# Norm sums by products with ones, rotary sums and 24 convolution taps a layer by accumulating transfers, in a two-layer hybrid encoder

## The chip, the cores and the metric

The kernel runs on one core of a Trainium2 chip. The metric is the device time of one execution in microseconds. A core has a matrix engine (TensorE, PE in the profile, PEld for its weight loads), three elementwise engines (VectorE is DVE, ScalarE is ACT, GpSimd is POOL), and 16 DMA engines that are fed by queues; the queues here are SP's (SyncE), POOL's and, rarely, ScalarE's. Each engine works through its own instructions in order and waits on semaphores for the others.

## The reference

Two layers work on x (512 tokens by 1024 channels, float32). Cut to what matters:

```python
h = rmsnorm(x, norm_mix[i])
proj = h @ w_in[i]
qa, ka, va, glu_in, qc, kc, vc, gates = split(proj)
ya = diff_attention(qa, ka, va, ...)      # 4 heads, rotary embedding on q and k, rmsnorm per head
yb = conformer_conv(glu_in, ...)          # gate, 31-tap depthwise convolution, layernorm, silu
yc = neighbourhood_attention(qc, kc, vc, rpb)
ga, gb, gc = split(sigmoid(gates))
x = x + (ga * (ya @ w_br_a) + gb * (yb @ w_br_b) + gc * (yc @ w_br_c)) @ w_o
h = rmsnorm(x, norm_ffn[i])
x = x + (silu(h @ w_ffn_gate) * (h @ w_ffn_up)) @ w_ffn_down
h = rmsnorm(x, norm_ple[i])
x = x + sigmoid(h @ w_ple_gate) * (p[i] @ w_ple_in)
# after both layers: rmsnorm(x, norm_final)

def apply_rope(x, cos, sin):
    x1, x2 = x[..., :half], x[..., half:]
    rot = concatenate([-x2, x1])
    return x * cos + rot * sin
```

## The kernel before

Activations lie transposed: channels on the 128 partitions, the 512 tokens along the row. Every float32 operand of a large product is split into a high and a low part (`split`: ScalarE copies the high part, VectorE subtracts it for the low part, lines L147 and L161), and one product is three matmuls, high by high, high by low and low by high (L181 to L183). Weights come in tiles of 128x1024 on SP's queue, are split the same way, and have three buffers for each of raw, high and low (tags `wr`, `wh`, `wl`).

TensorE's order is written out by hand; the order on the other engines is made by a scheduler from priorities. A counter of product chunks (`chunk`, `tick`) drives generators: attention units, norms and the convolution's end are resumed so many ticks later (`yield n`, `later`), so that their few matmuls lie between those of the large products.

A norm (`norm`, L207 to L233) takes a tile of squares `sq`, 128 partitions by 512 tokens. Four transposes (L217) put tokens on the partitions, VectorE reduces along the row (L220), a small VectorE instruction scales the sum, POOL raises it to the power -0.5 (L227), and after some ticks four more transposes (L231) broadcast the result over the partitions. It is called for each of the six main norms, for the eight heads' norms and for the convolution's two.

The rotary embedding (`diff_in`, L831 on) takes the projection of a head's queries or keys: ScalarE copies it out of PSUM into `raw`, four transfers on SP's queue (L846) write the swapped 32-partition blocks into `rot`, VectorE multiplies `raw` by the cosine table in place and `rot` by the sine table and adds them. Then the sum is split, and `stack` (L664) copies 64-partition pieces into the layout of the scores, four transfers for queries and eight for keys, on SP's queue.

The convolution has 31 taps for each of 4 channel blocks, one VectorE instruction each (`taps`, L164 with `conv_z`). `background` puts so many taps behind given instructions of other stages; the numbers are in `BG` (per call, by stage). The convolution's sums `cs` are finished by `conv`, which begins after `merge_a`.

The order of a layer: `glu` (gate of the convolution), neighbourhood attention's projections and units, the differential attention's `diff_in`, `diff_v` and units, the gates `gate_c`, the branch `branch_c`, `merge_a`, `gate_b`, `merge_b`, the output projection `w_o`, the FFN and the per-layer input. In the FFN, POOL already issues accumulating transfers (L1004), which add weight blocks from DRAM to a tile in SBUF.

Of the kernel before, what the change touches and what calls it, by code (L numbers as in the profile page):

```python
# [14 lines left out]
AF = mybir.ActivationFunctionType  # L15
ALU = mybir.AluOpType
AX = mybir.AxisListType
# [3 lines left out]
P = 128  # L21
# [3 lines left out]
GR = 8  # L25
# [5 lines left out]
CON3W = 31  # L31
# [14 lines left out]
PAR_L = 8 + 8 + 8 + 1 + 4 + 4 + 4 + 4 * CON3W  # L46
PAR = L * PAR_L + 8
WARM = 8
BG = dict(glu=2, natten=1, values=3, diff=1, gatec=2, branchc=2, gateb=4, mergea=4, mergea2=2)
FIRST = (["v"] * 4 + ["pt"] * 2 + ["y", "b"], ["y"] * 5 + ["pt"] * 2 + ["b"])  # L50
EARLY = 6
QUARTERS = (2, 4, 6)
# [13 lines left out]
class Net:  # L66
# [143 lines left out]
    def norm(self, sq, n, waits, done, spread=True, eps=None):  # L210


        nc = self.nc
        yield waits[0]
        st = self.ps("tr", (P, 4, P))
        for c in range(4):
            nc.tensor.transpose(st[:, c, :], sq[:, c * P:(c + 1) * P], self.ident)  # L217
        with self.tc.high_priority(offset=min(200, self.tc.cur_priority - self.p0) if n == D and self.p0 is not None else 0):
            sm = self.sb("sm", [P, 4])
            nc.vector.tensor_reduce(out=sm, in_=st, op=ALU.add, axis=AX.X)  # L220
            ms = self.sb("sm", [P, 4])
            if eps is None:
                nc.vector.tensor_scalar(ms, sm, 1.0 / n, EPS, ALU.mult, ALU.add)
            else:
                self.stt(ms, sm, 1.0 / n, eps, ALU.mult, ALU.add)
            col = self.sb("rc", [P, 4])
            nc.gpsimd.tensor_tensor(col, ms, self.power, ALU.pow)  # L227
        yield waits[1]
        bc = self.ps("tr", (P, 4, P))
        for c in range(4):  # L230
            nc.tensor.transpose(bc[:, c, :], col[:, c:c + 1].to_broadcast([P, P]), self.ident)  # L231
        bc = bc.rearrange("p a b -> p (a b)")
        done(col, self.spread(bc) if spread else bc)  # L233
# [198 lines left out]
    def layer(self, i, h, xsrc, xs):  # L432
        self.i, self.h = i, h
        zs, cs = [], []
        self.todo = self.taps(zs, cs)
        self.glu(zs)
        if i == 0:
            self.lambdas()
        yc, ya, yb = [], [], []
        sn, sd = {}, {}  # L440
        self.natten_in(0, sn, yc)
        self.drain(self.renorm)
        self.h = self.hs
        self.natten_v(sn)
        last = self.glu_last(zs)
        self.natten_in(1, sn, yc)
        next(last)
        self.natten_in(2, sn, yc)
        next(last)
        self.natten_in(3, sn, yc)  # L450
        acc, gb = [], []
        self.diff_in(0, sd, ya)
        self.diff_v(0, sd)
        self.diff_in(1, sd, ya)
        self.gate_c(acc, 0)
        self.diff_in(2, sd, ya)
        self.diff_v(1, sd)
        self.diff_in(3, sd, ya)
        for m in range(1, KD):
            self.gate_c(acc, m)  # L460
        for m in range(2):
            self.gate_b(gb, m, AF.Copy, None)
        for g in acc + gb:
            self.act(g, g, AF.Sigmoid, table="sigmoid")
        self.branch_c(acc, yc)
        for m in range(2, 4):
            self.gate_b(gb, m, AF.Sigmoid, "sigmoid")
# [12 lines left out]
        h = self.ffn(h, x)  # L480
        return self.ple(h, x, xs, self.inputs())
# [57 lines left out]
    def taps(self, zs, cs):  # L539

        for j, z in enumerate(zs):
            zf = z.rearrange("p a b -> p (a b)")
            c = self.sb("z", [P, 512])
            cs.append(c)
            for d in range(CON3W):
                w = self.par(self.i, "cw", j * CON3W + d)
                src = zf[:, d * GR:d * GR + 512]
                if d == 0:
                    yield self.nc.vector.tensor_scalar(c, src, w, self.par(self.i, "cb", j),
                                                       ALU.mult, ALU.add)  # L550
                else:
                    yield self.stt(c, src, w, c, ALU.mult, ALU.add)

    def background(self, after, n):

# [223 lines left out]
    def gate_c(self, acc, m):  # L779
        self.phase = "gatec"  # L780
        ps = self.proj(OFF_G + 2 * D + m * P)
        if m % 2 == 0:
            acc += self.parts_of("x", [512], 2)
        self.background(self.act(acc[m], ps, AF.Copy), self.bg["gatec"])

    def branch_c(self, acc, ys):
        self.phase = "branchc"
        for m in range(KD):
            ps = self.ps("mm")
            self.gemm(ps, self.a["w_br_c"][self.i, m], ys)  # L790
            self.background(self.tt(acc[m], acc[m], ps, ALU.mult), self.bg["branchc"])

    def merge_a(self, ys, acc):
        self.phase = "mergea"
        for m in range(KD):
            ps = self.proj(OFF_G + m * P)
            g = self.sb("t", [P, 512])
            self.background(self.act(g, ps, AF.Sigmoid, table="sigmoid"), self.bg["mergea"])
            pb = self.ps("mm")
            self.gemm(pb, self.a["w_br_a"][self.i, m], ys)  # L800
            self.tt(g, g, pb, ALU.mult)
            self.background(self.tt(acc[m], acc[m], g, ALU.add), self.bg["mergea2"])

    def gate_b(self, gs, m, func, table):
        self.phase = "gateb"
        ps = self.proj(OFF_G + D + m * P)
        if m % 2 == 0:
            gs += self.parts_of("v", [512], 2)
        self.background(self.act(gs[m], ps, func, table=table), self.bg["gateb"])

    def merge_b(self, ys, acc, gs):
        self.phase = "mergeb"
# [17 lines left out]
    def diff_in(self, head, st, ys):  # L830
        self.phase = "diff"  # L831
        if head == 0:
            st["tabs"] = []
            for t in range(2):
                c = self.sb("r", [P, 512])
                self.nc.sync.dma_start(c, self.a["rope"][t])
                st["tabs"].append(c)
        st4 = self.sb("qk", [P, 4, 512], F32R)
        k2 = self.sb("x", [P, 2, 512], F32R)
        for s, off in enumerate((OFF_QA, OFF_KA)):  # L840
            ps = self.proj(off + head * P)
            raw, rot = self.sb("rp", [P, 512]), self.sb("rp", [P, 512])
            self.act(raw, ps, AF.Copy, scale=1.0 if s else 0.125)
            for b in range(4):
                o = b ^ 1
                self.nc.sync.dma_start(rot[32 * b:32 * b + 32], raw[32 * o:32 * o + 32])  # L846
            self.background(self.tt(raw, raw, st["tabs"][0], ALU.mult), self.bg["diff"])
            self.tt(rot, rot, st["tabs"][1], ALU.mult)
            self.tt(raw, raw, rot, ALU.add)
            nat, low = self.sb("kh", [P, 512], F32R), raw.bitcast(F32R)  # L850
            self.split(nat, low, raw)
            self.stack(nat, low, st4[:, 2 * s:2 * s + 2], k2 if s else None)
        box = dict(s0=self.sb("sm", [P, 4]))
        for qt in range(4):
            self.later(self.diff_unit(head, qt, st4, k2, st, box, ys), 6 if head else 7, 2)
# [538 lines left out]
def _token_order():  # L1394
    t = np.arange(S)
    return (t % GR) * GW + t // GR


def _rope_tables():
    inv = np.float32(1.0) / (10000.0 ** (np.arange(0, 64, 2) / 64)).astype(np.float32)  # L1400
    ang = np.arange(S, dtype=np.float32)[:, None] * inv[None, :]
    ang = np.concatenate([ang, ang], axis=-1)
    cos, sin = np.cos(ang), np.sin(ang)
    sin[:, :32] = -sin[:, :32]
    n = _token_order()
    return np.ascontiguousarray(
        np.stack([np.concatenate([c[n].T, c[n].T], axis=0) for c in (cos, sin)])).astype(np.float32)

# [75 lines left out]
```

## Time and profile before

| | us |
|---|---|
| median of 3 runs | 1768.67 (1768.25 to 1769.67) |
| span of the profiled execution, first to last instruction; the page states no other time of it | 1766.6 |
| TensorE busy | 1759.3 |
| VectorE busy | 1408.6 |
| ScalarE busy | 885.5 |
| POOL busy | 98.4 |

The granted clock of TensorE is 1.000 over the span. A row of the page's groups gives line, engine, operation, tile written and tiles read, the shape, the count, then busy time in us, the mean in ns, and idle time before with what ended it. The waits name who waited for whom, with total, count and longest in us. A timeline row begins with start and length in us.

### The profile page before, as it was taken

Reading aid. Unit: us, or ns where it says so; the run is one execution under the profiler, and the core shown is the slowest. Engines: PE = TensorE matmul, PEld = TensorE weight load, DVE = VectorE, ACT = ScalarE, POOL = GpSimd, SP = SyncE. Lnnn points to the kernel's source line nnn. Section 1 sums busy time; section 2 is a strip of 40 time slices with the busy share of each in tenths; the row PEclk is TensorE's granted clock in tenths of the full one; section 3 lists DMA queues with packets and bytes.
Section 4 is the critical chain, followed back from the end, with each engine's and each line's share of the span. In section 5 each row is a group of like instructions: output and inputs, shape, how many; then the busy total and the mean of one; then the engine's idle time right before and its main releaser. Section 6 shows DMA issues by size and latency. Waiting matters only on the chain.

```text
span 1766.6 us, 27127 instructions
## 1 busy us (share of the span) xinstructions
PE 1759.3 (100%) x10146; PEld 1551.8 (88%) x10146; DVE 1408.6 (80%) x2354; ACT 885.5 (50%) x1529; POOL 98.4 (6%) x114
## 2 busy tenths in 40 slices
PE   9999999999999999999999999999999999999998
PEld 7888888888899899998888888888888998989987
DVE  7967988998898587787777688889887976867776
ACT  5576555325565254454545655552356643534444
POOL 0000000000111010100000000000001110101000
PEclk9999999999999999999999999999999999999999
DMA  6575641334757365544446655322356674655332
GB/s 231 158 186 160 162 123 54 102 100 150 222 153 196 106 173 156 137 126 127 151 137 173 180 148 154 108 73 94 101 183 194 168 179 118 172 141 156 99 104 96
DMA packets 112548, 253.95 MB, mean 144 GB/s; under 512 B 14368, under 2 KB 23328, under 8 KB 112416
## 3 DMA queue, kind: packets, MB, share of 16 engines
q1 hardware_dynamic: 99024, 227.83, 42.0%
q0 software_dynamic: 12672, 23.07, 8.1%
q8 instruction: 80, 1.31, 0.3%
q10 hardware_dynamic: 720, 1.31, 0.2%
q14 instruction: 52, 0.43, 0.1%
HBM read 214.41 MB, written 7.34 MB: 126 GB/s over the span
## 4 chain that ended last, share of the span: by engine, by line
PE 92%; DVE 4%; DMA 2%; ACT 2%; issue 1%; SPq 0%; POOL 0%; ACTq 0%; POOLq 0%; DVEq 0%
PE ffn_mm L1034 4%; PE ffn_mm L1036 4%; PE ffn_mm L182 4%; PE ffn_mm L181 4%; PE ffn_mm L183 4%; PE ffn_mm L1035 4%; PE ffn_sc L1036 3%; PE ffn_sc L1034 3%; PE ffn_sc L1035 3%; PE mergea_mm L182 2%; PE mergea_mm L183 2%; PE mergea_mm L181 2%; PE gateb_mm L182 2%; PE gateb_mm L183 2%; PE gateb_mm L181 2%; PE wo_mm L182 2%
## 5 line engine op out<-in xcount | busy, mean ns | idle before, releaser
L164 DVE SCALAR_TENSOR_TENSOR conv_z<-glu_z,pre_par,conv_z 128x512 f32<-128x512 f32 x240 | 179.6, 748 | 3.5
L147 ACT ACTIVATE ffn_wh<-ffn_wr 128x1024 fp32r<-128x1024 f32 (+1 forms) x92 | 92.8, 1015 | 111.9 <-PE ffn_mm L182 81.4
L1004 POOL DMA_DIRECT2D ffn_qk<-w_fu x88 | 78.1, 978 | 605.6 <-DMA ffn_qk<-w_fu 289.7
L161 DVE TENSOR_TENSOR ffn_wl<-ffn_wr,ffn_wh 128x1024 fp32r<-128x1024 f32 (+1 forms) x92 | 107.4, 1173 | 5.3 <-ACT ffn_wh L147 4.6
L161 DVE TENSOR_TENSOR ffn_t<-ffn_mm,wo_rb 128x512 f32<-128x512 f32 (+1 forms) x64 | 38.7, 605 | 68.4 <-PE ffn_mm L183 68.4
L147 ACT ACTIVATE mergea_wh<-mergea_wr 128x1024 fp32r<-128x1024 f32 (+1 forms) x32 | 27.1, 848 | 96.8 <-PE mergea_mm L182 79.5
L147 ACT ACTIVATE ffn_wh<-ffn_qk 128x1024 fp32r<-128x1024 f32 x44 | 46.7, 1061 | 37.1 <-PE ffn_mm L182 15.9
L161 DVE TENSOR_TENSOR ffn_wl<-ffn_qk,ffn_wh 128x1024 fp32r<-128x1024 f32 x44 | 53.9, 1224 | 10.7 <-ACT ffn_wh L147 10.7
L161 DVE TENSOR_TENSOR ffn_t<-ffn_t,ffn_t 128x512 f32<-128x512 f32 (+1 forms) x46 | 31.3, 680 | 31.9 <-ACT ffn_t L147 31.4
L147 ACT ACTIVATE natten_e<-natten_e,natten_s 128x192 f32<-128x192 f32 (+1 forms) x88 | 39.3, 474 | 25.2 <-DVE natten_s L726 21.9
L181 PE MATMUL ffn_mm<-ffn_v,ffn_wh 128*128 128x512 f32 x132 | 51.4, 389 | 0.0
L182 PE MATMUL ffn_mm<-ffn_v,ffn_wh 128*128 128x512 f32 x132 | 51.4, 389 | 0.0
L183 PE MATMUL ffn_mm<-ffn_v,ffn_wl 128*128 128x512 f32 x132 | 51.3, 389 | 0.0
L181 PE MATMUL ffn_mm<-ffn_y,ffn_wh 128*128 128x512 f32 x132 | 51.3, 389 | 0.0
L182 PE MATMUL ffn_mm<-ffn_y,ffn_wh 128*128 128x512 f32 x132 | 51.3, 389 | 0.0
L183 PE MATMUL ffn_mm<-ffn_y,ffn_wl 128*128 128x512 f32 x132 | 51.3, 389 | 0.0
L147 ACT ACTIVATE diff_a<-diff_sc,diff_s 128x512 f32<-128x512 f32 x32 | 22.0, 687 | 57.1 <-DVE diff_s L919 57.0
L1036 PE MATMUL ffn_mm<-wo_h,ffn_wl 128*128 128x256 f32 x176 | 49.8, 283 | 0.0
L1036 PE MATMUL ffn_sc<-wo_h,ffn_wl 128*128 128x256 f32 x176 | 49.8, 283 | 0.0
L1035 PE MATMUL ffn_sc<-wo_h,ffn_wh 128*128 128x256 f32 x176 | 49.8, 283 | 0.0
L1035 PE MATMUL ffn_mm<-wo_h,ffn_wh 128*128 128x256 f32 x176 | 49.8, 283 | 0.0
L1034 PE MATMUL ffn_sc<-wo_h,ffn_wh 128*128 128x256 f32 x176 | 49.8, 283 | 0.0
(879 smaller groups left out, 6539.8 us busy)
## 6 DMA issues: line engine op xcount, KB each, us to landing
ffn_qk<-w_fu POOLq DMA_DIRECT2D x88, 256.0 KB, 5.7
ffn_wr<-w_fg SPq DMA_DIRECT2D x44, 512.0 KB, 3.7
ffn_wr<-w_fd SPq DMA_DIRECT2D x32, 448.0 KB, 4.1
ffn_r<-w_fu SPq DMA_DIRECT2D x44, 256.0 KB, 4.2
ffn_qk<-w_fg SPq DMA_DIRECT2D x44, 256.0 KB, 4.0
ffn_qk<-w_fu SPq DMA_DIRECT2D x44, 256.0 KB, 4.2
natten_wr<-w_in SPq DMA_DIRECT2D x16, 512.0 KB, 4.3
diff_wr<-w_in SPq DMA_DIRECT2D x16, 512.0 KB, 4.2
```

Source lines behind the costliest of these rows:

```text
L147: i = self.nc.scalar.activation(out, in_, func, **kw)
L161: return self.nc.vector.tensor_tensor(out, a, b, op)
L164: return self.nc.vector.scalar_tensor_tensor(out, a, s, b, op0, op1)
L181: mm(out, wh, ah, start=first, stop=False)
L182: mm(out, wh, al, start=False, stop=False)
L183: mm(out, wl, ah, start=False, stop=last)
L1004: nc.gpsimd.dma_start(q, wu[:, lo], accum_op=ALU.add)
L1034: mm(out, wh[:, c], bh, start=first and k == 0, stop=False, skip_group_check=True)
L1035: mm(out, wh[:, c], bl, start=False, stop=False, skip_group_check=True)
L1036: mm(out, wl[:, c], bh, start=False, stop=k == 3, skip_group_check=True)
```

## The change

Three edits, and new counts for the background taps.

- In `norm`, the four transposes become four matmuls with the squares as the stationary tile and one column of ones as the moving one, so PSUM holds the four columns of sums; the reduction is dropped.
- In `diff_in`, `rot` becomes the product of `raw` with a sine table whose halves are exchanged, `raw` is multiplied by the cosine table in place, and four transfers issued by POOL add the swapped blocks of `rot` to `raw`.
- Of the convolution's channel blocks 2 and 3, the first 12 taps each leave VectorE. ScalarE writes the first product with the bias into one of two `b` buffers (`self.far`), and the other 11 products into `t` tiles, which POOL's transfers add to it. `link` takes the next of these 24 steps a layer; it is called in the attention, gate, branch and merge stages. The remaining taps run on VectorE as before, on top of that sum.

```diff
-BG = dict(glu=2, natten=1, values=3, diff=1, gatec=2, branchc=2, gateb=4, mergea=4, mergea2=2)
+BG = dict(glu=2, natten=1, values=3, diff=1, gatec=2, branchc=1, gateb=2, mergea=3, mergea2=2)
+LINKS = 24
...
     def norm(...):
         yield waits[0]
-        st = self.ps("tr", (P, 4, P))
+        sm = self.ps("tr", (P, 4))
         for c in range(4):
-            nc.tensor.transpose(st[:, c, :], sq[:, c * P:(c + 1) * P], self.ident)
+            nc.tensor.matmul(sm[:, c:c + 1], sq[:, c * P:(c + 1) * P], self.ones[:, 0:1],
+                             start=True, stop=True)
         with self.tc.high_priority(...):
-            sm = self.sb("sm", [P, 4])
-            nc.vector.tensor_reduce(out=sm, in_=st, op=ALU.add, axis=AX.X)
...
     def layer(...):
-        self.todo = self.taps(zs, cs)
+        self.todo, self.links = self.taps(zs, cs), self.chain(zs)
...
         self.diff_in(2, sd, ya)
+        self.link()
         self.diff_v(1, sd)
+        self.link()
         self.diff_in(3, sd, ya)
+        self.link()
...
     def taps(self, zs, cs):
-            c = self.sb("z", [P, 512])
+            if j < 2:
+                c, n = self.sb("z", [P, 512]), 0
+            else:
+                for _ in self.links:
+                    pass
+                c, n = self.far[j - 2], LINKS // 2
             cs.append(c)
-            for d in range(CON3W):
+            for d in range(n, CON3W):
...
+    def chain(self, zs):
+        self.far = [self.sb("b", [P, 512]) for _ in range(2)]
+        for n in range(LINKS):
+            d, j = divmod(n, 2)
+            w = self.par(self.i, "cw", (j + 2) * CON3W + d)
+            src = zs[j + 2].rearrange("p a b -> p (a b)")[:, d * GR:d * GR + 512]
+            if d == 0:
+                self.act(self.far[j], src, AF.Identity, scale=w, bias=self.par(self.i, "cb", j + 2))
+            else:
+                t = self.sb("t", [P, 512])
+                self.act(t, src, AF.Copy, scale=w)
+                self.nc.gpsimd.dma_start(self.far[j], t, accum_op=ALU.add)
+            yield
...
+        self.link()          # also in gate_c, branch_c, merge_a and gate_b, once per block
...
     def diff_in(...):
             self.act(raw, ps, AF.Copy, scale=1.0 if s else 0.125)
+            self.tt(rot, raw, st["tabs"][1], ALU.mult)
+            self.background(self.tt(raw, raw, st["tabs"][0], ALU.mult), self.bg["diff"])
             for b in range(4):
                 o = b ^ 1
-                self.nc.sync.dma_start(rot[32 * b:32 * b + 32], raw[32 * o:32 * o + 32])
-            self.background(self.tt(raw, raw, st["tabs"][0], ALU.mult), self.bg["diff"])
-            self.tt(rot, rot, st["tabs"][1], ALU.mult)
-            self.tt(raw, raw, rot, ALU.add)
+                self.nc.gpsimd.dma_start(raw[32 * b:32 * b + 32], rot[32 * o:32 * o + 32],
+                                         accum_op=ALU.add)
...
     def _rope_tables():
         sin[:, :32] = -sin[:, :32]
+        sin = np.concatenate([sin[:, 32:], sin[:, :32]], axis=-1)
```

More of the change, by code (lines that the diff above doesn't have):

```diff
@@ L552, in taps, with link @@
                     yield self.stt(c, src, w, c, ALU.mult, ALU.add)
+    def chain(self, zs):
[11 more added lines that the diff above has]
+            yield
+    def link(self):
+        ph, self.phase = self.phase, "conv"
+        next(self.links, None)
+        self.phase = ph
     def background(self, after, n):
@@ L791, in branch_c @@
             self.background(self.tt(acc[m], acc[m], ps, ALU.mult), self.bg["branchc"])
+            self.link()
     def merge_a(self, ys, acc):
@@ L798, in merge_a @@
             self.background(self.act(g, ps, AF.Sigmoid, table="sigmoid"), self.bg["mergea"])
+            self.link()
             pb = self.ps("mm")
@@ L809, in gate_b @@
         self.background(self.act(gs[m], ps, func, table=table), self.bg["gateb"])
+        self.link()
     def merge_b(self, ys, acc, gs):
```

## The prediction, made blind

> **What bounds the kernel now.** I read the page first (busy shares, then the shares of the chain that ended last), then the waits of TensorE alone, then windows of 20 us, and last the timeline around the blocks that change.
>
> ```profile
> span 1766.6 us, 27127 instructions
> PE 1759.3 (100%) x10146; PEld 1551.8 (88%) x10146; DVE 1408.6 (80%) x2354; ACT 885.5 (50%) x1529; POOL 98.4 (6%) x114
> PE 92%; DVE 4%; DMA 2%; ACT 2%; issue 1%; SPq 0%; POOL 0%; ACTq 0%; POOLq 0%; DVEq 0%
> PE pre_av L329 <- DVE pre_zeror L402: 1.1, 1, 1.1
> PE natten_av L763 <- DVE natten_a L161: 0.3, 1, 0.3
> ```
>
> TensorE is busy for 1759.3 of 1766.6 us, and all its listed waits together are 1.4 us. VectorE is busy 80% of the span, and 4% of the chain runs through it, which looks like 70 us to be had. A busy TensorE is not proof of full pace, since ends of matmuls are modelled. So I compare counts of matmuls in windows where VectorE is nearly full with one where it is half idle:
>
> ```profile
> 60.00:80.00 20.00, 20.00 (x91) 16.61 (x90) 19.33 (x26) 9.38 (x13) 0.00 (x0) 1.00 0.55 162
> 340.00:360.00 20.00, 20.00 (x90) 16.57 (x89) 18.76 (x27) 4.74 (x7) 0.00 (x0) 1.00 0.32 93
> 580.00:600.00 20.00, 20.00 (x90) 16.56 (x89) 11.53 (x14) 5.21 (x5) 0.00 (x0) 1.00 0.33 105
> ```
>
> The columns are the length, then busy time and count of TensorE, its weight loads, VectorE, ScalarE and POOL, then the granted clock. TensorE starts 91, 90 and 90 matmuls in 20 us whether VectorE is busy 19.33, 18.76 or 11.53 us, at a granted clock of 1.00. One matmul per 0.22 us is its own pace. Where the chain runs through VectorE, VectorE is the last to be ready, but TensorE still has work in front of it. So a microsecond taken off VectorE is not a microsecond off the span, and an instruction added to TensorE is.
>
> **Part 1: sums of the norms.** L217 transposes a 128x512 tile of squares in four pieces and L220 reduces them on VectorE. There are 16 such norms:
>
> ```profile
> L220 DVE TENSOR_REDUCE diff_sm<-diff_tr x8: 679/684/692, 213.9 to 1181.0; 128x4 f32<-128x512 f32 x8
> L220 DVE TENSOR_REDUCE conv_sm<-conv_tr x2: 684/685/686, 409.9 to 1284.9; 128x4 f32<-128x512 f32 x2
> L220 DVE TENSOR_REDUCE wo_sm<-wo_tr x2: 682/684/687, 495.3 to 1370.3; 128x4 f32<-128x512 f32 x2
> L220 DVE TENSOR_REDUCE ffn_sm<-ffn_tr x2: 691/692/692, 839.2 to 1714.2; 128x4 f32<-128x512 f32 x2
> L220 DVE TENSOR_REDUCE glu_sm<-glu_tr x1: 691/691/691, 27.4 to 27.4; 128x4 f32<-128x512 f32 x1
> L220 DVE TENSOR_REDUCE ple_sm<-ple_tr x1: 692/692/692, 889.1 to 889.1; 128x4 f32<-128x512 f32 x1
> ```
>
> The change drops 16 reductions of 0.684 us (10.9 us of VectorE) and replaces the 64 transposes by 64 products of the same stationary tile with one column of ones. That very product stands in the kernel already, once, in the last stage (L1339), so its price can be read beside that of the transposes:
>
> ```profile
> 494.38 0.28 PE L1036 MATMUL ffn_mm<-wo_h,ffn_wl 128*128 128x256 f32 x1
> 494.50 0.60 PE L217 MATMUL wo_tr<-pre_ident,wo_ss 128*128 128x128 f32 x4
> 494.86 0.36 PE L1034 MATMUL ffn_mm<-wo_h,ffn_pt 128*128 128x256 f32 x1
> 495.06 0.28 PE L1035 MATMUL ffn_mm<-wo_h,ffn_pt 128*128 128x256 f32 x1
> ...
> 1749.19 0.28 PE L1275 MATMUL ple_mm<-ple_wh,ffn_z 128*128 128x256 f32 x1
> 1749.31 0.95 PE L1339 MATMUL ple_mm<-pre_ones,ple_ss 128*128 128x1 f32 x8
> 1750.12 0.42 PE L1280 MATMUL ple_tr<-pre_ident,ple_h 128*128 128x128 f32 x2
> 1750.37 0.38 PE L1280 MATMUL ple_tr<-pre_ident,wo_x 128*128 128x128 f32 x2
> 1750.51 0.36 PE L1273 MATMUL ple_mm<-ple_wh,ffn_z 128*128 128x256 f32 x1
> 1750.71 0.28 PE L1274 MATMUL ple_mm<-ple_wl,ffn_z 128*128 128x256 f32 x1
> ```
>
> Columns: start, length, engine, line, tiles, form and count. A 256-column step is 0.12 us (494.38 to 494.50). From 494.38 to 495.06 two such steps and four transposes pass: 0.68 - 0.24 = 0.44 us for the transposes. L1339 writes four products and the trace has eight matmuls for them: each float32 product is two passes, and each pass loads the 128 columns of squares anew. From 1749.19 to 1750.71 pass two 256-column steps, eight passes and four transposes: 1.52 - 0.24 - 0.44 = 0.84 us for the eight. So a norm costs TensorE 0.84 - 0.44 = 0.40 us more. The start-to-start distances instead (1749.31 to 1750.12 = 0.81, against 494.50 to 494.86 = 0.36) give 0.45. Sixteen norms: 6.4 to 7.2 us. I take the middle, 6.8. Nothing hides it, because TensorE has no idle time at these places, and the shorter way to the norm's factor moves nothing, because the transposes of that factor (L231) stand at a fixed place in TensorE's order with other products between.
>
> The row of L1339 has one weight load for every pass, 0.1 us apart, though only one column is streamed. [...]
>
> **Part 2: 24 convolution taps a layer, and the background counts.** VectorE loses 48 of these:
>
> ```profile
> L164 DVE SCALAR_TENSOR_TENSOR conv_z<-glu_z,pre_par,conv_z 128x512 f32<-128x512 f32 x240 | 179.6, 748 | 3.5
> L1004 POOL DMA_DIRECT2D ffn_qk<-w_fu x88: 865/883/1247, 449.3 to 1635.3; - x88
> DMA to landing us min/median/max: 3.6/5.7/9.2
> L147 ACT ACTIVATE diff_rp<-diff_mm x16: 577/592/612, 139.6 to 1100.6; 128x512 f32<-128x512 f32 x16
> L147 ACT ACT_TABLE_LOAD x13 | 16.7, 1283 | 1.4 <-PEq L1473 1.2
> ```
>
> 48 x 0.748 = 35.9 us of VectorE. ScalarE gains 48 products, priced by its 128x512 copy at 0.59 us: 28 us on an engine that is half idle. Four of them use a function (Identity) that the trace of before does not show: between nothing and two table loads of 1.28 us each time, 10 us of ScalarE at most; I take nothing, as the cover is the same. POOL gains 44 accumulating transfers; the kernel has such ones in the FFN (L1004, 0.883 us of POOL each, 5.7 us to landing). The window at 340 us shows what all this is worth to the span: zero, as TensorE holds 90 matmuls per 20 us. Background slots fall from 128 to 104 a layer against 100 taps left, so the last tap still falls inside the merge with the attention branch. Cover that could fail: the first tap of block 2 on VectorE follows in program order behind the last link, so VectorE may stand for one ScalarE product, one issue and one landing (0.6 + 0.9 + 5.7 = 7 us at the most), with weight splits queued behind it. One 1024-column weight tile feeds 24 matmuls of 0.22 us (5.3 us), and three tiles are buffered, so about two tiles of work lie ahead. I cost it at nothing. Both `b` buffers are held by the sums until the convolution ends; their next use is in the quarters of the output projection, after that.
>
> **Part 3: rotary sums.** Per head and side, VectorE loses one addition (16 x 0.69 = 11 us), four partition swaps leave SP's queue, and four accumulating transfers enter POOL's, behind both products. Here latency counts. The tightest case is the keys of the second head:
>
> ```profile
> 174.01 0.59 ACT L147 ACTIVATE diff_rp<-diff_mm 128x512 f32<-128x512 f32 x1
> 180.46 1.87 SPq L846 DMA_DIRECT2D diff_rp<-diff_rp  x3
> 187.38 0.69 DVE L161 TENSOR_TENSOR diff_rp<-diff_rp,diff_rp 128x512 f32<-128x512 f32 x1
> 192.53 1.24 SPq L664 DMA_DIRECT2D diff_x<-diff_rp  x2
> diff_x<-diff_rp SPq DMA_DIRECT2D x16, 128.0 KB, 2.4
> 197.29 0.40 PE L828 MATMUL diff_sc<-diff_qk 128*128 128x512 f32 x1
> ```
>
> Now the sum is ready at 188.07, 13.5 us after the copy ends at 174.60; three swaps waited in SP's queue until 180.46. The last stacking transfer is issued about 193.1 and lands 2.4 us later, at 195.5, and the scores that need it start at 197.29: 1.8 us to spare. Afterwards: two products of 0.69, up to 4 us of other VectorE work between, four POOL issues of 0.88, and a landing between 3.6 and 9.2 us after the last issue. That is 1.4 + 2.6 + 3.6 = 7.6 us at best, 5.4 + 2.6 + 5.7 = 13.7 us with a full VectorE queue and the median landing, 17.2 us at worst, against 13.5 + 1.8 = 15.3 us that are allowed. I take a value at or below the median case, since these transfers carry 64 KB and L1004's carry 256 KB from DRAM: no stall, and no gain beyond the listed waits.
>
> **The sum.** Span 1766.6 + 6.8 = 1773.4 us. The page gives the profiled execution no other time than its span. The median of the runs, 1768.67, lies 2.07 above it, which I carry over: **1775.5 us**. From below, the 6.4 and all 1.4 us of listed waits gone give 1773.7, and the lowest run, 0.4 under the median, 1773.2.
>
> **Rivals.**
> *POOL holds up a norm (slower still).* The power of a norm's factor (L227) runs on POOL, in order, now between links:
>
> ```profile
> 307.53 1.43 POOL L227 TENSOR_TENSOR diff_rc<-diff_sm,pre_power 128x4 f32<-128x4 f32 x1 [29.30 <-PE branchc_mm L182]
> 309.99 0.58 PEld L231 LDWEIGHTS diff_tr<-pre_ident,diff_rc 128*128 128x128 f32 x4
> ```
>
> The fourth head has 1.0 us between the end of the power (308.96) and its use (309.99). Links then come once per branch block (12 matmuls, 2.7 us), and each waits for the landing of the one two before it, 5.4 us earlier. With 0.9 + 5.7 us per link POOL waits 1.2 us, which the dropped reduction covers; with 9.2 us it waits 4.7, and TensorE stands about 3.4 us in each layer. The point is a landing above 6 us. Price 2 to 7 us: 1777.5 to 1782.5.
> *Rotary sums land late (slower still).* Above 15.3 us for the keys of the first two heads, up to 1.9 us each, four times: up to 7.6 us, 1777 to 1783.
> *The products are hidden (faster).* If the passes ran at the pace of their one column, under the matmuls next to them, their price would fall from 0.84 toward 0 and the transposes' 0.44 x 16 = 7.0 us would be saved: 1761.6. The kernel is faster from under 0.44 us for the eight passes, and visibly so (3.5 us over 16 norms) from under 0.22. Against it stand the eight weight loads of L1339, 0.1 us apart. [...]
> *Passes share a load (no change).* If the two passes of a product need one load, the norm costs what four transposes cost: 1768.7. The same row speaks against it.
>
> **How the numbers follow.** Forecast 0.74, POOL's order 0.11, rotary 0.07, shared loads 0.05, hidden products 0.03. A measurement of this kernel can tell about 0.2% (3.5 us) from no change. Slower: 0.74 + 0.11 + 0.07 = 0.92; same 0.05; faster 0.03. The range runs from 1773.2 to 1782.5 and holds the forecast and nearly all of the two slower rivals.
>
> **What would show it.** Right: VectorE about 58 us less busy (35.9 + 11 + 10.9), TensorE with 64 matmuls more and its listed waits still about 1 to 2 us, the sums at L217's place as eight passes over 0.8 us. Wrong: a wait of TensorE on diff_qk, diff_x or the factor of a norm, or matmul counts per 20 us under 90 in the gate and branch stages; or a span that grew less than 6 us with the eight passes in place.

## The result, and the profile after

The changed kernel takes 1800.74 us (median of four runs, 1797.29 to 1802.57) against 1769.05 for the kernel before on the same chip (1768.25 to 1769.67). The ratio is 1.0177, 95% interval 1.0163 to 1.019: 31.7 us slower, where 1775.5 was forecast and 1782.5 was the upper end of the range. The direction was right and the size was not.

The page of the changed kernel, the same three lines as before, then a 20 us window in the same columns, then the head of TensorE's waits (total in us, times, longest):

```profile
span 1800.8 us, 27426 instructions
...
PE 1779.0 (99%) x10210; PEld 1567.9 (87%) x10210; DVE 1358.4 (75%) x2274; ACT 913.4 (51%) x1577; POOL 188.2 (10%) x222
...
PE 39%; DVE 1%; ACT 1%; DMA 0%; issue 0%; POOL 0%; ACTq 0%; POOLq 0%; DVEq 0%
```

```profile
340.00:360.00 20.00, 20.00 (x90) 16.56 (x89) 15.51 (x22) 4.84 (x7) 0.00 (x0) 1.00 0.51 133
```

```profile
PE natten_mm L792 <- ACT diff_rp L148: 5.8, 2, 2.9
PE natten_mm L792 <- DVE natten_a L162: 5.0, 2, 3.4
PE gateb_mm L182 <- ACT gateb_wh L148: 1.4, 2, 0.9
PE pre_av L329 <- DVE pre_zeror L402: 1.1, 1, 1.1
PE gateb_mm L184 <- DVE gateb_wl L162: 1.1, 2, 0.5
PE diff_mm L182 <- DVE diff_v L162: 0.6, 1, 0.6
PE natten_av L792 <- DVE natten_a L162: 0.5, 2, 0.3
```

VectorE is 50.2 us less busy (58 were foreseen) and TensorE has the 64 matmuls more that were foreseen. The chain's shares cannot be set beside those of before: they add up to some 41% of the span, because the chain is followed back only to the second layer. Where TensorE has work it still starts 90 matmuls in 20 us. What is new is the list of waits: 15.5 us in these seven lines, against 1.4 in the list of before. The largest two are waits of the neighbourhood attention for ScalarE and VectorE, and both are in the stretch where the rotary sums are made.

The third item is the clock. Five stretches of 3.41 us around the first long wait, in the columns of the windows (length; busy time and count of TensorE, its weight loads, VectorE, ScalarE, POOL; granted clock; DMA share; GB/s):

```profile
146.94:150.36 3.42, 3.42 (x31) 3.42 (x29) 0.50 (x1) 0.00 (x0) 0.49 (x1) 1.00 0.68 186
150.36:153.77 3.41, 0.21 (x2) 0.01 (x1) 0.98 (x2) 1.67 (x3) 0.00 (x0) 1.00 0.02 2
153.77:157.18 3.41, 3.22 (x15) 3.23 (x16) 3.35 (x6) 0.77 (x2) 1.30 (x3) 0.50 0.66 154
157.18:160.60 3.42, 3.42 (x18) 3.42 (x18) 2.67 (x10) 1.04 (x4) 1.84 (x3) 0.50 0.93 196
160.60:164.00 3.40, 3.40 (x31) 3.40 (x30) 0.69 (x1) 1.56 (x5) 0.00 (x0) 1.00 0.19 34
```

TensorE stands in the second stretch (0.21 us busy), and for the next 6.83 us it works at clock 0.50: 15 and 18 matmuls in place of 31. There are three such pairs in the execution, from 153.77, 184.49 and 1075.37 us; before had none between its start and its end. Each costs at most half of 6.83 us, since TensorE also waits for a part of it; together that is up to 10.2 us.

So of the 34.2 us by which the span grew, 14.1 are waits in these lines (15.5 less 1.4), up to 10.2 are half clock, and 7.2 are the norms' passes (16 times the 0.45 us below): 31.5. The other 2.7 us are not placed; the list has two more lines, of 0.5 us together.

### The profile page after: what moved, and what is told of

Read it like the earlier page. It is cut to its first block, busy times and chain, and to the rows that moved or that the text cites. A ratio compares the mean times of both kernels' runs of the same rounds, so it can differ in the third digit from the quotient of the medians.

```text
span 1800.8 us, 27426 instructions
## 1 busy us (share of the span) xinstructions
PE 1779.0 (99%) x10210; PEld 1567.9 (87%) x10210; DVE 1358.4 (75%) x2274; ACT 913.4 (51%) x1577; POOL 188.2 (10%) x222
## 3 DMA queue, kind: packets, MB, share of 16 engines
q8 instruction: 80, 1.31, 0.3%
q10 hardware_dynamic: 720, 1.31, 0.2%
## 5 line engine op out<-in xcount | busy, mean ns | idle before, releaser
L165 DVE SCALAR_TENSOR_TENSOR conv_z<-glu_z,pre_par,conv_z 128x512 f32<-128x512 f32 x120 | 89.5, 746 | 1.1
L881 POOL DMA_DIRECT2D diff_rp<-diff_rp x64 | 51.0, 1214 | 357.2 <-PE natten_tr L767 127.1
L165 DVE SCALAR_TENSOR_TENSOR conv_b<-glu_z,pre_par,conv_b 128x512 f32<-128x512 f32 x76 | 56.8, 749 | 1.5
L574 POOL DMA_DIRECT2D conv_b<-conv_t x44 | 39.0, 918 | 174.3 <-ACT conv_t L148 112.5
L162 DVE TENSOR_TENSOR ffn_t<-ffn_t,ffn_t 128x512 f32<-128x512 f32 (+1 forms) x46 | 31.3, 679 | 32.0 <-ACT ffn_t L148 31.5
L1068 PE MATMUL ffn_sc<-wo_h,ffn_wh 128*128 128x256 f32 x176 | 49.8, 283 | 0.0
```

What stands on the lines that cost most here:

```text
L162: return self.nc.vector.tensor_tensor(out, a, b, op)
L165: return self.nc.vector.scalar_tensor_tensor(out, a, s, b, op0, op1)
L574: self.nc.gpsimd.dma_start(self.far[j], t, accum_op=ALU.add)
L881: self.nc.gpsimd.dma_start(raw[32 * b:32 * b + 32], rot[32 * o:32 * o + 32], accum_op=ALU.add)
L1068: mm(out, wh[:, c], bl, start=False, stop=False, skip_group_check=True)
```

## Experiments

**Norms alone.** The first edit of the diff by itself; everything else as before.

> The kernel before with only the norms' sums changed. All theories agree on the mechanism here and differ in size: by weight loads (eight passes at 0.113 us against four transposes at 0.109) each of 16 norms costs TensorE 0.46 us, so +7.4 us, about 1776.4. A rival, that the norms also bring part of the large loss by their shorter path on VectorE or POOL, would give over 1780.

1775.62 us (ratio 1.004, 1.0025 to 1.0055): +6.7, and TensorE's only waits over 0.2 us are the two of before. The forecast of 1775.5 is in effect the time of this kernel. The timeline of the changed kernel at the same norm as in the prediction:

```profile
512.60 0.95 PE L218 MATMUL wo_tr<-pre_ones,wo_ss 128*128 128x1 f32 x8
513.41 0.36 PE L1067 MATMUL ffn_mm<-wo_h,ffn_pt 128*128 128x256 f32 x1
```

Eight passes take 0.81 us from start to next start, as L1339's did, against 0.36 for four transposes.

**One pass for each product.** ScalarE rounds the squares first, and the products are of the rounded tile with two columns of ones:

```diff
+        sqr = self.sb("t", [P, 512], F32R)
+        self.act(sqr, sq, AF.Copy)
...
+            nc.tensor.matmul(two[:, c, :], sqr[:, c * P:(c + 1) * P], self.ones_r[:, 0:2], ...)
```

> The kernel before with the norms' sums by products with two columns of ones, of squares that ScalarE has rounded to float32r, so that each product is one pass with one weight load. It changes the precision of the sums. Theory (the price of the norms is the second pass's weight load, 64 times 0.113 us): four passes cost what four transposes cost, and the time is that of before, 1768 to 1770.5. Rival (a product with ones is dearer than a transpose whatever its passes): 1775.

1771.71 us (1.0015, 1.0006 to 1.0025), 1.2 above the upper end. Its timeline at that norm:

```profile
496.73 0.57 PE L220 MATMUL wo_tr<-pre_onesr,wo_t 128*128 128x2 f32 x4
497.16 0.36 PE L1036 MATMUL ffn_mm<-wo_h,ffn_pt 128*128 128x256 f32 x1
```

Four passes take 0.43 us, near the 0.36 of the transposes, so it is the number of passes that a norm pays for. The 2.5 us that stay fit 16 times the 0.07 us between them and short waits behind the added ScalarE copy, which were not taken apart: the list names diff_tr behind `ACT diff_t` (1.0 us) and two waits on VectorE (0.9 and 0.7), none of which norms alone had.

**Rotary sums alone.** The edit in `diff_in` with the exchanged sine table.

> The kernel before with only the rotary sums changed. Theory: the sum of the queries lands late, ScalarE and VectorE stand in order before its split, and the copies and splits queued behind them keep TensorE waiting in the first two heads of each layer; about +21 us (some 11 us of standing and three stretches of 6.8 us at half clock), 1788 to 1792. Rival: the loss needs the links on POOL's queue beside it; then rotary alone stays within 3 us of before, 1766 to 1772.

1789.87 us (1.0118, 1.0103 to 1.0133): +21.0, with no links and no norms changed, so that the rival which needed the links falls. TensorE's two longest waits, and ScalarE's timeline around the first sum (start, length; in brackets the idle time before and its releaser):

```profile
PE natten_mm L763 <- ACT diff_rp L147: 5.7, 2, 2.9
PE natten_mm L763 <- DVE natten_a L161: 5.2, 2, 3.3
```

```profile
151.51 0.63 ACT L147 ACTIVATE diff_kh<-diff_rp 128x512 fp32r<-128x512 f32 x1 [7.14 <-DMA diff_rp<-diff_rp]
152.04 0.36 ACT L147 ACTIVATE natten_a<-natten_tr 64x256 fp32r<-64x256 f32 x1
```

The same place in the kernel before:

```profile
147.15 0.38 ACT L147 ACTIVATE natten_a<-natten_tr 64x256 fp32r<-64x256 f32 x1 [3.50 <-DVE natten_pt L161]
147.75 0.63 ACT L147 ACTIVATE diff_kh<-diff_rp 128x512 fp32r<-128x512 f32 x1 [0.22 <-DMA diff_wr<-w_in]
```

Before, the split of the rotated queries (`diff_kh`) ran at 147.75 with its sum there. Now the sum is in flight until 151.5, ScalarE stands 7.14 us in front of the split, and the attention's split (`natten_a`), for which TensorE waits, has been put behind it in ScalarE's order. The 3.42 us from 151.22, of which TensorE is busy for 1.27, are followed by 3.41 us at clock 0.50; the mean granted clock of the execution is 0.996.

Over the whole execution ScalarE's standing in front of this split is, with the rotary sums and then before (total, times, longest):

```profile
ACT diff_kh L147 <- DMA diff_rp<-diff_rp: 30.3, 8, 7.1
```

```profile
ACT diff_kh L147 <- DVE diff_rp L161: 17.4, 8, 4.2
```

ScalarE stood there before, too, with 1.4 us of listed waits of TensorE in all. So it is not any standing that costs, but one so long that the work queued behind it comes late for TensorE.

**A plain swap of the products.** The order of the change (products first), but SP swaps the sine product into a free tile and VectorE adds it. Against the rotary edit, cut to the lines that matter:

```diff
-                self.nc.gpsimd.dma_start(raw[...], rot[...], accum_op=ALU.add)
+                self.nc.sync.dma_start(swap[32 * b:32 * b + 32], rot[32 * o:32 * o + 32])
+            self.tt(raw, raw, swap, ALU.add)
```

> The kernel before with the rotary products made first, as in the change, but the swap of the product by four plain transfers on SP's queue into another tile and the addition on VectorE. Theory (it is the 6 to 7 us that POOL's four accumulating transfers need, after the products, that makes the queries' sum 4 us later): the sum is ready about 2 us later than before at the most, TensorE stands 0 to 2 us in a layer and keeps its clock; 1769 to 1775. Rival (it is the products ahead of the transfer, not POOL): as the rotary change alone, 1787 to 1791.

1773.97 us (1.0025, 1.0014 to 1.0035). The split of the queries runs at 145.61 in place of 151.51, the wait on `natten_a` at L763's `natten_mm` is gone, and one wait is left that before did not have:

```profile
PE natten_mm L763 <- ACT diff_rp L147: 4.6, 2, 2.6
```

The time is as expected, the clock is not: one stretch of 6.83 us at half clock, from 1052.88, follows the second layer's wait. So 16 of the 21 us go with the accumulating transfers. This does not yet tell their lateness from the transfers themselves.

**The split later, and its order forced.** First the split and the stacking of a rotated tile were emitted some ticks later on the whole change. Then, for the rotary edit alone and for the whole change, the split was also ordered behind the attention's split and the latest copy. Last the same with more ticks:

```diff
-            self.split(nat, low, raw)
-            self.stack(nat, low, st4[:, 2 * s:2 * s + 2], k2 if s else None)
+            self.run(self.summed(raw, st4[:, 2 * s:2 * s + 2], k2 if s else None))
...
+    def summed(self, raw, one, two):
+        yield DEFER                          # 3, later 4 for keys and 6 for queries
...
+        self.behind(i, self.pe_hi)           # from the second version on
+        self.behind(i, self.copied)
```

The whole change, later by 3 ticks:

> The changed kernel, with the split and the stacking of each rotary sum issued three ticks (24 products of three matmuls would be two ticks, so about 8 us) later in program order, so that the copies and splits of the attention units stand ahead of it on ScalarE and VectorE. Theory (ScalarE and VectorE stand in order before a sum that has not landed): the waits on natten_a and on the copy of the keys go, and with them the stretches of half clock; the scores have 5 to 7 us to spare; 1800.7 less 16 to 20 us, 1780 to 1785. Rival (the sums are late for the scores, whatever the order): the wait moves to the scores and the time stays at 1795 or more.

1799.38 us (1.0171, 1.0156 to 1.0187). A miss: the scheduler, which orders ScalarE by priorities, put the split back at the same place (151.15, after 6.30 us of standing, with `natten_a` behind it), so the edit did not do what it was for.

The rotary edit alone and the whole change, with the order forced:

> The kernel before with the rotary change, its split issued three ticks later, and an order forced on ScalarE and VectorE: the split of a rotary sum stands behind the latest split of an attention unit (natten_a) and behind the latest copy out of a projection (that of the keys, for the queries' sum). The transfers are as late as in the rotary change alone. Theory (the loss is the order: engines standing before a sum with ready work behind it): the two long waits of each layer go, no stretch of half clock is left, 1769 to 1774 against 1789.9. Rival (the sums are too late for what needs them): over 1782, with the wait on diff_qk or diff_x.

> The same forced order in the full changed kernel. Theory: what is left is the norms' 7 us and the links' 3 to 7, so 1778 to 1784 against 1800.7. Rival: over 1792.

1787.04 (1.0105, 1.009 to 1.012) and 1797.92 us (1.0165, 1.0148 to 1.0182): both above what the theory gave and in their rivals' ranges, though the wait on diff_qk or diff_x that the first rival named does not show. ScalarE's timeline of the rotary edit with forced order:

```profile
146.01 0.38 ACT L148 ACTIVATE natten_a<-natten_tr 64x256 fp32r<-64x256 f32 x1 [1.85 <-DVE natten_pt L162]
151.26 0.63 ACT L148 ACTIVATE diff_kh<-diff_rp 128x512 fp32r<-128x512 f32 x1 [4.87 <-DMA diff_rp<-diff_rp]
```

`natten_a` now comes first and TensorE's wait for it is gone, but ScalarE still stands 4.87 us, and TensorE waits later instead, for `natten_e` (2.4 us), `diff_e` (1.4) and the copy of the keys `diff_rp` (4.7). In the rotary edit alone the forced order gave back 2 of 21 us: which instruction is next in line behind the split matters little.

With more ticks, alone and in the whole change:

> Rotary change alone (sums of squares by transposes and the convolution's adds on VectorE, as before), with the split of a head's rotated tile put off: the keys' split by four ticks, the queries' by six, and the order written out so that nothing of the attention unit stands behind a split whose sum has not landed. Theory (ScalarE and VectorE standing some 5 us in front of a sum still in flight is what costs): the split is issued after the landing, the standing before the first query split falls from about 5 us to under 1 us, TensorE's waits for the attention's split and for the copy of the keys go, and with them the half clock: 1769 to 1775 us. Rival (the sums themselves come too late for the scores): the later split makes the scores late, TensorE waits for the stacked queries or keys, and the time stays above 1783 us.

> The whole change with the same late splits. Theory: norms with their products and links with theirs stay as measured together (1781.7 us), and the rotary part falls to 0 to 3 us: 1778 to 1785 us. Rival (sums too late for the scores, or the three parts cost more together): above 1793 us.

1784.48 (1.0089, 1.0072 to 1.0106) and 1799.07 us (1.0169, 1.0154 to 1.0184). Both are outside what the theory gave and in the rivals' ranges (above 1783 and 1793), but without the rival's waits on diff_qk or diff_x. ScalarE still stood 4.40 us in front of the first split. These runs left the theory untested, since none had taken the standing away.

**POOL does the split.** This takes the wait out of ScalarE's and VectorE's queues and leaves transfers, issues and their lateness as they are. The lines of the rotary edit that change:

```diff
-            self.split(nat, low, raw)
+            self.nc.gpsimd.tensor_copy(nat, raw)
+            self.nc.gpsimd.tensor_tensor(low, raw, nat.bitcast(F32), ALU.subtract)
```

> Rotary change alone, with its accumulating transfers as they are, but the split of a head's rotated tile (the rounded copy and the subtraction) done by POOL instead of ScalarE and VectorE, so that neither of these two has anything in its queue that waits for the sum. Theory (the standing of ScalarE and VectorE in front of a sum in flight is what costs): TensorE's waits for the attention's split and for the copy of the keys out of PSUM go, and with them the half clock: 1768 to 1775 us, POOL's own slower split being hidden as long as the scores don't wait. Rival (the accumulating transfers themselves: POOL's issues, their traffic, or sums late for the scores): 1783 us or more, with waits of TensorE on diff_qk or diff_x if it is lateness.

1770.01 us, ratio 1.0005 (0.9995 to 1.0014): the rotary edit costs nothing that can be measured. POOL's timeline around the first sum, and all of TensorE's waits:

```profile
142.98 3.38 POOL L848 DMA_DIRECT2D diff_rp<-diff_rp  x4 [113.34 <-ACT diff_rp L147]
151.15 0.61 POOL L851 CAST diff_kh<-diff_rp 128x512 fp32r<-128x512 f32 x1 [4.80 <-DMA diff_rp<-diff_rp]
151.85 1.30 POOL L852 TENSOR_TENSOR diff_rp<-diff_rp,diff_kh 128x512 fp32r<-128x512 f32 x1
```

```profile
PE pre_av L329 <- DVE pre_zeror L402: 1.1, 1, 1.1
PE diff_sc L828 <- ACT diff_e L147: 0.8, 2, 0.5
PE natten_mm L763 <- ACT diff_rp L147: 0.4, 1, 0.4
PE natten_av L763 <- DVE natten_a L161: 0.3, 1, 0.3
```

The sum is as late as ever (151.15) and an engine stands 4.80 us for it, but it is POOL, which has nothing else to do there. No wait on diff_qk or diff_x shows: the sums were never late for the scores. So what cost is that ScalarE and VectorE stood in front of a sum in flight, and the transfers, their issues and their traffic are free here. The edit also takes the work of 16 splits off ScalarE and VectorE. With that work left where it was the plain swap cost 4.7 us, so the work can be no more than that of the 21 us.

**Later without POOL.** The plain swap with a second transfer of the whole tile in front of the add (`self.nc.sync.dma_start(rot, swap)`):

> The plain swap of the products on SP's queue with VectorE's add (1773.97 us), with a second transfer of the whole tile behind the swap, ahead of the add, so that the sum is some 2.5 to 4 us later and POOL has no part in it. Theory (a later sum in front of in-order engines costs, whoever moves it): 1777 to 1788 us, between the plain swap and the accumulating transfers (1789.9), with TensorE's waits on the attention's split or on the copy of the keys back. Rival (the accumulating transfers or POOL are to blame, not the lateness): within 2 us of 1774.

1780.52 us (1.0062, 1.0046 to 1.0079), 6.6 above the plain swap. ScalarE's wait for the sum and TensorE's waits:

```profile
151.83 0.63 ACT L147 ACTIVATE diff_kh<-diff_rp 128x512 fp32r<-128x512 f32 x1 [5.53 <-DVE diff_rp L161]
```

```profile
PE diff_sc L828 <- ACT diff_e L147: 3.2, 2, 1.6
PE natten_av L763 <- DVE natten_a L161: 2.8, 3, 1.2
PE natten_mm L763 <- ACT diff_rp L147: 1.4, 2, 0.7
```

Lateness alone, with no accumulating transfer of these sums, brings the waits back. They are shorter than in the rotary edit, none over 1.6 us (10.5 us in the whole list against 14.6), and the mean granted clock of this execution is 1.000, where that of the rotary edit is 0.996, some 7 us of its 1788.0. With the 4.1 us less of waits that is about the 9.7 us between this run's 11.3 and the 21. The total of ScalarE's standing is no measure of the cost: in front of the split it stood 17.4 us here, as before, but 5.5 us at the longest.

**Links alone, and with the norms.** The third edit with its counts of taps, first by itself, then with the first edit.

> The kernel before with only the convolution links and the new background counts. Theory: two waits of a gate's weight split behind products of links, about 2 us in each layer, so +3 to +4.5 us, 1772 to 1773.5, with no stretch of half clock. Rival (the links are the cause of the large loss): over +15 us. Rival (VectorE's relief gains): below 1768.

1775.84 us (1.0045, 1.0028 to 1.0062), above the expected range, and the wait is another one:

```profile
PE diff_tr L232 <- POOL diff_rc L228: 4.1, 2, 2.0
```

```profile
307.58 0.86 POOL L575 DMA_DIRECT2D conv_b<-conv_t  x1 [2.16 <-DMA conv_b<-conv_t]
309.82 0.87 POOL L575 DMA_DIRECT2D conv_b<-conv_t  x1 [1.38 <-DMA conv_b<-conv_t]
310.38 1.71 POOL L228 TENSOR_TENSOR diff_rc<-diff_sm,pre_power 128x4 f32<-128x4 f32 x1
```

POOL stands for landings of earlier links, and the fourth head's power runs at 310.38 in place of 307.53: the rival "POOL holds up a norm". A stretch of half clock follows it (3.41 us from 312.19, of which 1.7 us are lost).

> The changed kernel with the rotary sums undone. Theory: the parts add, so 1768.9 + 7.4 + 4 = 1780, and the granted clock stays at full pace between the first and the last microseconds. Rival (the parts interact, as through POOL's order): 1790 or more.

1781.69 us (1.0069, 1.0054 to 1.0084), as expected. With the reduction dropped the power is in time, and another wait takes its place:

```profile
PE gateb_mm L182 <- ACT gateb_wh L148: 2.7, 2, 1.9
...
PE gateb_mm L184 <- DVE gateb_wl L162: 1.1, 2, 0.5
```

In the whole change the reason stands in ScalarE's waits for links, and in its timeline just ahead of `gate_b`:

```profile
ACT conv_t L148 <- DMA conv_b<-conv_t: 15.8, 12, 2.7
```

```profile
332.52 0.72 ACT L148 ACTIVATE conv_t<-glu_z,pre_par 128x512 f32<-128x512 f32 x1 [2.70 <-DMA conv_b<-conv_t]
333.81 0.72 ACT L148 ACTIVATE conv_t<-glu_z,pre_par 128x512 f32<-128x512 f32 x1 [0.57 <-DMA conv_b<-conv_t]
334.44 1.99 ACT L148 ACTIVATE gateb_wh<-gateb_wr 128x1024 fp32r<-128x1024 f32 x2
```

A link's product waits for the landing that frees its tile, and the split of gate_b's weights is queued behind it.

**Links earlier.** Two links in each `gate_c` call and none in the branch:

> The links-only kernel, with two links per gate_c block and none in the branch stage, so that none is under way on POOL when the fourth head's norm needs its power. Theory (the cost of the links alone is the power of that norm behind links on POOL, 2 us in each layer and a stretch of half clock): the waits on POOL go, 1768.5 to 1771. Rival (links cost wherever they stand, on ScalarE's queue): 1774 to 1779.

1774.9 us (1.0033, 1.0021 to 1.0044; single runs 1772.6 to 1778.01): the profiled execution has no wait on POOL's power, but the time is above the expected 1768.5 to 1771 and in the rival's 1774 to 1779. Yet the rival's cause, ScalarE's queue, has shrunk: ScalarE stands 3.4 us for links in place of 16.7. Moving the links moved TensorE's waits (natten_y 1.2 us, diff_pt 1.1), and what this run pays stays open.

**POOL does the split, in the whole change; then the links' products too.**

> The whole change, with the split of the rotated tile done by POOL as in the run above. Theory: norms by products and links together measured 1781.7 us; the rotary part adds 0 to 4 us: 1781 to 1787 us, unless POOL's queue, which now holds links, rotary transfers, splits and the norms' powers, holds up a norm's factor (then a wait of TensorE behind POOL's power shows, and up to 1792). Rival (the transfers themselves cost): 1795 us or more.

1781.55 us (1.0072, 1.0057 to 1.0087): the time of norms and links, with the same two waits on gate_b's weights (2.6 and 1.0 us). The rotary sums add nothing here either. Then `self.act(...)` in `chain` became `self.nc.gpsimd.tensor_scalar(...)`:

> The whole change, with POOL doing the split of the rotated tile and the links' products too, so that neither ScalarE nor VectorE has an instruction in its queue that waits for the landing of an accumulating transfer, but for the first tap behind the chain. Theory (standing in front of landings is what the links cost as well): TensorE's waits for the split of gate_b's weights go, and the time falls from 1781.6 us to that of the norms alone, 1774.5 to 1778 us. Rival (POOL's order in front of a norm's factor, now with the products' time on POOL too): a wait of TensorE behind L227's power, 1780 to 1790 us. Rival (the added transfers' traffic): 1781 or more with no such wait.

1778.26 us (1.0048, 1.0031 to 1.0064), 0.3 above the upper end. The waits on gate_b are gone, at 2.375 us for each product on POOL, and what is left, beside the two waits of before, is:

```profile
PE natten_mm L792 <- ACT diff_rp L148: 1.3, 1, 1.3
PE diff_sc L861 <- ACT diff_e L148: 1.1, 2, 0.5
```

```profile
L573 POOL TENSOR_SCALAR conv_t<-glu_z,pre_par 128x512 f32<-128x512 f32 x44 | 93.6, 2375 | 0.0
```

The same without the first edit (norms' sums by transposes):

> The links and the rotary sums with POOL doing the products and the split, and the norms' sums as before (transposes and a reduction on VectorE). Theory (POOL's order in front of a norm's factor is the wait that is left, as the reduction's 0.68 us stands in front of it again): a wait of TensorE behind the power of at most 4 to 5 us in all, 1770 to 1777 us. Rival (nothing is left): 1769 us, that of before.

1774.54 us (1.0039, 1.0026 to 1.0053; single runs 1772.63 to 1780.76), in the expected range, with the wait that was expected:

```profile
PE diff_tr L232 <- POOL diff_rc L228: 3.5, 2, 2.0
```

No version was faster than the kernel before. With TensorE short of no work there, the best of them (POOL's split with the rotary edit) equals it.

## Why the prediction was right and wrong

The increases, each over the kernel before on its own chip, add up in steps:

| kernel | us over before | step |
|---|---|---|
| norms alone | 6.7 | 6.7 |
| whole change, splits and products on POOL | 9.0 | 2.2 |
| products back on ScalarE | 12.4 | 3.4 |
| splits back on ScalarE and VectorE: the whole change | 31.7 | 19.3 |

- **What bounds the kernel: right, but half of the rule.** VectorE gave back 50 us and none came off the span; matmuls added to TensorE came on it in full. What was missing: an engine that is half idle can still stop TensorE, if an instruction in its queue waits. ScalarE is 51% busy in the changed kernel, and TensorE's largest wait, 5.8 us, is for it.
- **Part 1: right.** 6.8 forecast, 6.7 measured alone. The eight passes take the 0.81 us read from L1339. The rivals "products hidden" and "passes share a load" fall by the same row, and one pass for each product costs about what a transpose does (0.43 us for four against 0.36).
- **Part 2: wrong by about 6 us.** The links cost 7.0 us by themselves, and 6.1 on top of the norms (1781.69 against 1775.62 us). The step that failed is "I cost it at nothing". The cover was checked for one waiting instruction, the first tap on VectorE; the products on ScalarE were counted as busy time alone. But ScalarE's products wait for landings: 15.8 us of ScalarE's idle time in 12 waits, and the split of gate_b's weights stood behind them. Taking the products off ScalarE gave 3.4 us back; the rest stays open. The rival about POOL's order was a real mechanism: it is what links alone pay (4.1 us, and 3.5 in the last run). In the whole change the dropped reduction covers it, as the rival's own condition said.
- **Part 3: wrong, and most of the miss.** It was put at "no stall" and cost 21.0 us alone and 19.3 in the whole change. The durations were near: four issues in 3.4 us (foreseen 2.6, to the start of the last), and landings of 2.4, 3.3 and 6.7 us (least, median, most; foreseen 3.6, 5.7 and 9.2). The step that failed is the deadline, "against 13.5 + 1.8 = 15.3 us that are allowed". It ran to the scores, and for the scores the sums were in time. The first that waits for a sum is its split, an instruction in the queues of ScalarE and VectorE, and the deadline was that split's turn. The trace of before had it: `diff_kh` at 147.75, directly behind `natten_a`, for the queries of the first head. The products end at 143.40 in the changed kernel, which runs 1.2 us later there (its copy ends at 141.42 against 140.18). With the prediction's own 2.6 us of issues and 3.6 to 5.7 us to landing the sum comes at 149.6 to 151.7, which is 0.6 to 2.7 us past that turn; the split ran at 152.10. I took the keys of the second head for the tightest case because its slack to the scores was the least.
- **The clock: no term at all.** The granted clock was 1.00 in the rows, and the sum had no price for what follows when TensorE stands. It is up to 10.2 us of the 34.2 in the span.
- **Range and chances.** The rival "rotary sums land late" had the right edit and the wrong place, and was priced by its shortfall at the scores, 7.6 us at most. Both slower rivals were held to one wait each, without the clock. None of the waits named as signs of being wrong (diff_qk, diff_x, a norm's factor) shows in the changed kernel; what failed is the sign of being right, listed waits of 1 to 2 us.

What stays open: the 2.7 us of the span that are not placed, the 2.2 us between norms alone and the whole change with all waits on POOL (two waits of 1.3 and 1.1 us fit, but were not taken away), and why links moved earlier still cost 5.7 us.

## To carry to other kernels

When a step is turned into an asynchronous transfer, its deadline is the turn of the first instruction that reads its result in an engine's in-order queue, not the last use that TensorE needs; look up in the trace of before when that instruction ran and what is queued behind it. Moving only that waiting instruction to an engine with nothing else to do was worth 19 us here, with the transfer as late as before. And price a stop of TensorE above its own length: in the changed kernel each of the three 3.41 us steps of the clock in which TensorE stood 62% to 94% of the time was followed by 6.83 us at half clock, and in links alone one with 60% by 3.41 us.

## What the runs showed of the hardware

In the changed kernel the three stretches of half clock lie on one grid of 3.41 us: the second and the third begin 30.72 and 921.60 us after the first, which is 9 and 270 times 3.413, and each lasts two steps. In the steps ahead of them TensorE stood 94%, 62% and 68% of the time (busy for 0.21, 1.31 and 1.09 us), so none was idle as a whole; steps with 41% and 34% (2.03 us busy from 334.67, 2.26 from 1041.23) were followed by clock 1.00. From links alone, the step with the 2.0 us stop and the next one; then the second layer, where a stop of the same length falls across two steps:

```profile
308.78:312.19 3.41, 1.37 (x7) 0.79 (x5) 1.65 (x3) 1.24 (x2) 2.27 (x2) 1.00 0.99 245
312.19:315.60 3.41, 3.41 (x10) 2.85 (x11) 1.14 (x3) 1.96 (x3) 1.78 (x2) 0.50 0.98 239
...
1185.92:1189.33 3.41, 2.90 (x13) 2.06 (x11) 0.79 (x2) 1.72 (x3) 1.67 (x3) 1.00 1.04 230
1189.33:1192.74 3.41, 1.89 (x11) 1.64 (x12) 1.86 (x3) 1.10 (x2) 2.41 (x3) 1.00 1.00 210
```

With 1.37 us busy of 3.41 the next step is at 0.50, and the one after it at 1.00 again; with 2.90 the next is at 1.00. What followed the step with 1.89 is not shown. In the rotary edit a step with 63% standing (1.27 us busy from 151.22) was followed by 0.50 in the next, in the plain swap one with 62% (1.29 from 1049.47) by 0.50 in the next two. It is no strict rule: in the last 10 us of the kernel before, a step with 57% standing (1.46 us busy from 1759.38) was followed by one at 1.00.

The accumulating transfer of 64 KB between tiles in SBUF was issued in 3.4 us for the first four in the changed kernel and landed there 2.4 to 6.7 us after its issue, 3.3 in the median. The plain swap of the same size on SP's queue landed after 2.5 us in the median of the plain-swap run and after 3.4 (1.9 to 5.1) in the kernel before. The function that was new in this kernel, Identity, brought no table load: 13 before and 13 after.
